# A decoder layer on one Trainium2 core: moving one operand load and fixing the order of splits in the direct parts of the last product

## Chip, core and metric

The kernel runs on one core of one Trainium2 chip. The metric is the device time of one execution in microseconds (us). A core has five engines that matter here: PE (TensorE, matrix products), DVE (VectorE), ACT (ScalarE), POOL (GpSimd) and SP (SyncE); each works through a queue of its own, and DMA transfers are issued from the SP and POOL queues.

## What is computed

One layer with three token mixers, an output projection, then a SwiGLU feed-forward network (FFN), on 512 positions of width 2048, in float32. Only the FFN matters for the change:

```python
def swiglu(h, w_in, w_out):
    gate, up = jnp.split(h @ w_in, 2, axis=-1)
    return (jax.nn.silu(gate) * up) @ w_out
...
        x = x + mix.astype(x.dtype)
        x = x + swiglu(rmsnorm(x, norm2_g[l]), w_ffn_in[l], w_ffn_out[l]).astype(x.dtype)
    return rmsnorm(x, final_g)
```

The hidden width is 44 tiles of 128 (5632). `h @ w_in` is called the first product here, the product with `w_out` the second.

## The kernel before

**Split operands.** Every float32 operand x of a product is cast to a rounded `hi` (on ACT) and a remainder `lo = x - hi` (on DVE). A product tile is then three matmuls, hi·hi, hi·lo and lo·hi (`mm3`), so no matmul of a weight tile can finish before its ACT cast and its DVE subtraction.

**First product.** Hidden tiles 0 and 1 (`Direct`) come first, then the loop over `Unit(j)`, j = 2 to 43. A unit makes seven combined products (a Strassen-like scheme), p1, p5, p6, p3, p7, p2, p4 in that order, and its last instructions are, on ACT, the copy of the p4 result (L924), and on DVE the add (L925) and the multiply (L926). The activations of tiles 0, 1, 2, 19, 20, 21 and 38 to 43 go to DRAM as `actd`; those of tiles 3 to 18 and 22 to 37 go there as combined operands `opd[0]` and `opd[1]`.

**Second product.** It runs over the hidden tiles in this order:

- `rest(R0, 0)`: the direct part of hidden tiles 0, 1, 2. For each pair n, n+1 of the 16 output tiles a weight block `rw` is loaded, split by `w_split` into `wh` and `wl`, and used in 2 x 18 matmuls of 256 columns into the PSUM tiles `rb`. For this first part the result is copied into `acc` by ACT (L1026); later parts add to `acc` on DVE (L1028).
- `load_ops(0)`: 14 pieces of the combined operands, each a DMA `so<-opd` on the POOL queue, a cast (L1000, ACT) and a subtraction (L1001, DVE) into `fop`. Then eight times `second(q, 3)`: seven combined products each.
- `rest(R1, 19)`, `load_ops(1)`, eight times `second(q, 22)`: the same for the other half; here the result of `rest` is added on DVE.
- `load_rest(R2)` and `last(n, ...)`: the direct part of hidden tiles 38 to 43, with the final norm.

`load_rest(js)` loads activations: a DMA `st<-actd` on POOL, a cast to `ra` (L990, ACT) and a subtraction (L991, DVE).

**Buffers.** The raw weights `rw` and half of the raw weights of `second` share three buffers (tag `w`); `wh` and `wl` have three each; the staging tiles of the pieces alternate between tags `raw` (three) and `s` (two); the staging tiles of `load_rest` have two (`rs`) and one (`sm`); `fop` tiles take over the space of the units' operands in the order in which the last unit frees them.

**Order of the queues.** Nothing in this part of the program writes the order out by hand. A scheduler orders each engine's queue from data dependences, buffers and a priority by program order, so an instruction whose inputs are ready can be queued ahead of earlier ones of the program. The queues are worked through in the order so found. `tc.keep_in_program_order(ins)` adds one edge: `ins` is queued behind the instruction that stands just before it in the program on the same engine. It adds no wait of its own on that one's end, other than the place in the queue.

Of the kernel before, what the change touches and what calls it, by code (L numbers as in the profile page):

```python
# [8 lines left out]
F32 = mybir.dt.float32  # L9
F32R = mybir.dt.float32r  # L10
# [6 lines left out]
P = 128  # L17
# [6 lines left out]
TH = T // 2  # L24
GP = 8
R0 = (0, 1, 2)
S0 = 3
R1 = (19, 20, 21)
# [21 lines left out]
def group_of(j):  # L50
    return 0 if S0 <= j < S0 + 2 * GP else 1 if S1 <= j < S1 + 2 * GP else None
# [40 lines left out]
def trunk_kernel(  # L92
# [22 lines left out]
    act, dve, pool = nc.scalar, nc.vector, nc.gpsimd  # L115
# [42 lines left out]
    def mm3(out, lh, ll, rh, rl, start, stop, skip=False):  # L158
        pe.matmul(out, lhsT=lh, rhs=rh, start=start, stop=False, skip_group_check=skip)
        pe.matmul(out, lhsT=lh, rhs=rl, start=False, stop=False, skip_group_check=skip)  # L160
        pe.matmul(out, lhsT=ll, rhs=rh, start=False, stop=stop, skip_group_check=skip)
# [546 lines left out]
    wq = tc.alloc_tile_pool(name="wq", bufs=1)  # L708
    x1 = keep.tile([P, KT, T], F32, tag="k", name="x1")
    x1d = [dram.tile([P, T], F32, name=f"x1d{n}") for n in range(KT)]  # L710
    actd = {j: dram.tile([P, 2, TH], F32, name=f"actd{j}") for j in range(NH) if group_of(j) is None}
# [23 lines left out]
    def op_pair(pi, b):  # L735
        t = pair_tile(nop[0], f"op{pi}")
        nop[0] += 1
        act.copy(t[:, :, 0], b)
        dve.tensor_sub(t[:, :, 1], b, t[:, :, 0].bitcast(F32))
        ops[pi] = t  # L740
# [3 lines left out]
    def rms2(th):  # L744
        hs = HALF[th]
        pb = big.tile([P, T], F32, tag="b", name=f"rms2_{th}")[:, :TH]
        pe.matmul(pb, lhsT=onesD, rhs=sqb[:, hs], start=True, stop=True)
        act.activation(rs2[:, hs], pb, AF.Sqrt, bias=eps)
        dve.reciprocal(rs2[:, hs], rs2[:, hs])
# [37 lines left out]
    sm = wq.tile([P, 3 * TH], F32, tag="sm", name="sm")  # L787
# [70 lines left out]
    class Unit(Products):  # L858
# [61 lines left out]
        def p4(self):  # L920
# [9 lines left out]
            elif self.pos:  # L930
# [4 lines left out]
                dve.tensor_sub(pr[:, 3], pr[:, 1], pr[:, 5])  # L935
                pool.dma_start(opd[g][(self.j - (S0, S1)[g]) // 2], pr[:, 0:7])

    rms2(1)
    big.release()
    pz = tc.alloc_tile_pool(name="pz", bufs=2, space=PSUM)  # L940
# [14 lines left out]
    dve.tensor_sub(b21, b21, b11)  # L955
    op_pair(4, b21)
    for j in range(2, NH):
        u = Unit(j)
        u.load1()
        u.load3()  # L960
        u.load2()
        for st in ("p1", "p5", "p6", "p3", "p7", "p2", "p4"):
            getattr(u, st)()
# [4 lines left out]
    fops = {}  # L968
    for i, pi in enumerate((1, 2, 5, 3, 6, 7, 4)):
        fops[pi] = pair_tile(i, f"fop{pi}")  # L970
    PORDER = (1, 5, 6, 3, 7, 2, 4)
    nst = [0]

    def stage():
        nst[0] += 1
        tg, bufs = ("rs", 2) if nst[0] % 3 else ("sm", 1)
        return wq.tile([P, 2, TH], F32, tag=tg, bufs=bufs, name=f"st{nst[0]}")

    acts = {}

    def load_rest(js):
        for i, j in enumerate(js):
            st = stage()
            pool.dma_start(st, actd[j])
            if len(js) == 3:
                ra = wq.tile([P, 2, 2, TH], F32R, tag="ld", bufs=3, name=f"ra{j}")
                hi, lo = ra[:, 0], ra[:, 1]
            else:
                hi, lo = (fops[PORDER[e // 8]][:, e % 8] for e in (2 * i, 2 * i + 1))
            act.copy(hi, st)  # L990
            dve.tensor_sub(lo, st, hi.bitcast(F32))  # L991
            acts[j] = (hi, lo)

    def load_ops(g):
        for pi in PORDER:
            for i, tg, bufs in ((0, "raw", 3), (4, "s", 2)):
                st = wq.tile([P, 1024], F32, tag=tg, bufs=bufs, name=f"so{g}{pi}{i}").rearrange("p (a t) -> p a t", t=TH)
                pool.dma_start(st, opd[g][i:i + 4, :, pi - 1].rearrange("a p t -> p a t"))
                hi, lo = (fops[pi][:, i:i + 4, x] for x in range(2))
                act.copy(hi, st)  # L1000
                dve.tensor_sub(lo, st, hi.bitcast(F32))  # L1001

    def w_split(w, cols, name):
        wh = wp.tile([P, 1024], F32R, tag="wh", name=f"wh_{name}")[:, :cols]
        wl = wp.tile([P, 1024], F32R, tag="wl", name=f"wl_{name}")[:, :cols]
        act.copy(wh, w)
        dve.tensor_sub(wl, w, wh.bitcast(F32))
        return wh, wl

    def rest(js, base):  # L1010
        kw = len(js)
        for n in range(0, KT, 2):
            w = wp.tile([P, 1024], F32, tag="w", name=f"rw{base}_{n}")[:, :2 * kw * P]
            nc.sync.dma_start(w.rearrange("p (n c) -> p n c", n=2),
                              wf2[n:n + 2, :, base:base + kw].rearrange("n p k c -> p n (k c)"))
            wh, wl = w_split(w, 2 * kw * P, f"r{base}_{n}")
            for i in range(2):
                tg = "bbzyxzyx"[(n + i) % 8]
                b = {"b": p2, "z": pz}.get(tg, pa).tile([P, T], F32, tag=tg, name=f"rb{base}_{n}{i}")
                for h in range(2):  # L1020
                    for kk in range(kw):
                        c = slice((i * kw + kk) * P, (i * kw + kk + 1) * P)
                        ah, al = acts[js[kk]]
                        mm3(b[:, HALF[h]], wh[:, c], wl[:, c], ah[:, h], al[:, h], kk == 0, kk == kw - 1)
                if base == 0:
                    act.copy(acc[:, n + i], b)  # L1026
                else:
                    dve.tensor_add(acc[:, n + i], acc[:, n + i], b)  # L1028

    GW = GP * P  # L1030

    def second(q, base):
# [12 lines left out]
        def prod(pi, a, out, start, dst):  # L1045
            wh, wl = w_split(a, GW, f"s{nm}_{pi}")
            o = fops[pi]
            for k in range(GP):
                c = slice(k * P, k * P + P)
                mm3(out, wh[:, c], wl[:, c], o[:, k, 0], o[:, k, 1], start and k == 0, k == GP - 1, skip=True)  # L1050
            d = acc[:, dst[0], HALF[dst[1]]]
            dve.tensor_add(d, d, out)
# [22 lines left out]
                dve.tensor_add(acc[:, n], acc[:, n], xr)  # L1075
        prod(4, a22, bx, False, (n2, 0))

    load_rest(R0)
    rest(R0, 0)
    load_ops(0)  # L1080
    for q in range(KT // 2):
        second(q, 3)
        if q == 3:
            load_rest(R1)
    rest(R1, 19)
    load_ops(1)
    for q in range(KT // 2):
        second(q, 22)
    load_rest(R2)

    sqf = wq.tile([P, 1024], F32, tag="raw", bufs=3, name="sqf")[:, :T]
# [32 lines left out]
    def last(n, th):  # L1124
# [5 lines left out]
        if th is None:  # L1130
            wh, wl = w_split(w, LW, f"f{n}")
        else:
            m = n - WIDE
            both = fops[PORDER[2 + m // 2]].rearrange("p k w t -> p (k w t)")
            wh, wl = (both[:, (2 * (m % 2) + x) * LW:(2 * (m % 2) + x + 1) * LW] for x in range(2))
            if th == 0:
                act.copy(wh, w)
                dve.tensor_sub(wl, w, wh.bitcast(F32))
# [21 lines left out]
    for th in range(2):  # L1160
        for n in range(WIDE, KT):
# [3 lines left out]
            if th == 1 and n > WIDE:  # L1165
                f = 4 * (n - WIDE - 1)
# [75 lines left out]
```

## Time and profile before

| | us |
|---|---|
| median of 3 runs | 2120.89 (2120.11 to 2120.92) |
| the profiled execution | 2120.17 |
| its span in the trace | 2118.5 |

The span is what the trace covers; 1.7 us of the execution lie around it. PE is busy in nearly every slice of the page. In the trace, a matmul's record is longer than its turn, because matmuls overlap; the distance between the starts of neighbours is what one costs. A row that names an idle time in brackets says how long the engine stood still before it and what ended that. The granted clock (PEclk) is given as a share of 2.4 GHz, so 0.5 is 1.2 GHz.

### The profile page before, as it was taken

The numbers are of one execution on the slowest core, as the hardware profiler recorded it, in microseconds if no ns is written. First come the engines' busy times: TensorE is split into PE (matmuls) and PEld (weight loads), VectorE is DVE, ScalarE is ACT, GpSimd is POOL, SyncE is SP. The second block draws the span as 40 slices with busy tenths as digits, with TensorE's granted clock in tenths as the row PEclk, the third lists the DMA queues.
The fourth block names the chain that finished last, engine by engine and source line by source line (L and its number), as shares of the span: only waits on it lengthen the run. The fifth ranks groups of instructions, "written<-read, shape, count | busy, mean of one in ns | idle before, by whom it ended". The sixth has DMA issues, their size and how long they took to land.

```text
span 2118.5 us, 32060 instructions
## 1 busy us (share of the span) xinstructions
PE 2098.1 (99%) x12770; PEld 1887.8 (89%) x12770; DVE 1604.2 (76%) x2183; ACT 1055.0 (50%) x1467; POOL 113.3 (5%) x212
## 2 busy tenths in 40 slices
PE   9999999999999999999999999999999999999997
PEld 8988899888888898888888888888888999999997
DVE  6445655566576779888988888888888788887765
ACT  6334455566655555445445444444545534533344
POOL 3000000000012210000000000000001000200000
PEclk9999999999999999999999999999999999999999
DMA  6332222222277764343344343343335645643333
GB/s 212 85 108 81 73 75 92 70 70 80 70 241 232 239 195 163 122 137 135 119 135 141 113 137 127 125 137 132 129 120 162 196 132 156 214 151 100 108 93 115
DMA packets 87670, 281.90 MB, mean 133 GB/s; under 512 B 10544, under 2 KB 25056, under 8 KB 87520
## 3 DMA queue, kind: packets, MB, share of 16 engines
q1 hardware_dynamic: 73088, 228.75, 33.5%
q0 software_dynamic: 13216, 50.34, 7.0%
q8 instruction: 100, 1.64, 0.3%
q10 hardware_dynamic: 1216, 0.76, 0.1%
q14 instruction: 50, 0.41, 0.1%
HBM read 253.60 MB, written 26.21 MB: 132 GB/s over the span
## 4 chain that ended last, share of the span: by engine, by line
PE 86%; issue 9%; DVE 1%; DMA 1%; ACT 1%; POOL 0%; DVEq 0%; POOLq 0%; ACTq 0%
PE bx L70 16%; PE sx L70 9%; PE wo L70 8%; PE bz L70 8%; PE wsd L70 6%; PE sz L70 4%; PE wsg L70 4%; PE by L70 4%; PE b L70 3%; PE c L70 3%; PE rb L70 2%; PE sy L70 2%; PE a L70 2%; PE wsr L70 2%; PE wsu L70 2%
## 5 line engine op out<-in xcount | busy, mean ns | idle before, releaser
L70 PE MATMUL bx<-op,fh 128*128 128x512 f32 x1344 | 478.0, 395 | 1.1 <-ACT fh L811 1.1
L70 PE MATMUL bx<-op,fl 128*128 128x256 f32 x1344 | 379.3, 282 | 0.9 <-DVE fl L812 0.9
L70 PEld LDWEIGHTS bx<-op,fh 128*128 128x128 f32 x1344 | 252.4, 188 | 60.1 <-ACT fh L811 1.4
L811 ACT CAST fh<-s 128x1024 fp32r<-128x1024 f32 x168 | 176.9, 1053 | 191.9 <-PE bx L70 59.1
L70 PEld LDWEIGHTS bx<-op,fl 128*128 128x128 f32 x1344 | 253.1, 188 | 1.2 <-DVE fl L812 1.2
L70 PE MATMUL bz<-op,fh 128*128 128x512 f32 x672 | 240.5, 396 | 0.0
L812 DVE TENSOR_TENSOR fl<-s,fh 128x1024 fp32r<-128x1024 f32 x168 | 204.9, 1220 | 43.3 <-ACT fh L811 43.2
L811 ACT CAST fh<-f 128x1024 fp32r<-128x1024 f32 x126 | 132.5, 1052 | 167.2 <-PE bx L70 85.4
L70 PE MATMUL bz<-op,fl 128*128 128x256 f32 x672 | 189.5, 282 | 0.2 <-DVE fl L812 0.2
L70 PE MATMUL sx<-fop,wh_s 128*128 128x256 f32 x1024 | 185.0, 282 | 0.0
L70 PE MATMUL wo<-mxs,wh_o 128*128 128x512 f32 x512 | 180.3, 394 | 1.6 <-ACT wh_o L154 1.6
L812 DVE TENSOR_TENSOR fl<-f,fh 128x1024 fp32r<-128x1024 f32 x126 | 153.8, 1220 | 15.6 <-ACT fh L811 15.2
L70 PEld LDWEIGHTS sx<-fop,wh_s 128*128 128x128 f32 x1024 | 157.8, 189 | 0.0
L70 PEld LDWEIGHTS bz<-op,fh 128*128 128x128 f32 x672 | 126.3, 188 | 30.5
L70 PE MATMUL wo<-mxs,wl_o 128*128 128x256 f32 x512 | 144.7, 283 | 0.0
L70 PE MATMUL sx<-fop,wl_s 128*128 128x256 f32 x512 | 144.3, 282 | 0.0
L70 PEld LDWEIGHTS bz<-op,fl 128*128 128x128 f32 x672 | 126.6, 188 | 0.5 <-DVE fl L812 0.5
L70 PE MATMUL wsd<-xs,wh_d 128*128 128x512 f32 x384 | 122.8, 401 | 0.0
L70 PE MATMUL by<-op,fh 128*128 128x512 f32 x336 | 119.9, 397 | 0.0
L70 PEld LDWEIGHTS wo<-mxs,wh_o 128*128 128x128 f32 x512 | 96.2, 188 | 24.0 <-ACT wh_o L154 2.0
L70 PEld LDWEIGHTS sx<-fop,wl_s 128*128 128x128 f32 x512 | 96.8, 189 | 0.0
L70 PEld LDWEIGHTS wo<-mxs,wl_o 128*128 128x128 f32 x512 | 96.3, 188 | 0.5 <-DVE wl_o L155 0.3
(406 smaller groups left out, 4720.7 us busy)
## 6 DMA issues: line engine op xcount, KB each, us to landing
f<-wf SPq DMA_DIRECT2D x168, 512.0 KB, 3.9
w_o<-wout SPq DMA_DIRECT2D x36, 512.0 KB, 4.3
sraw<-wf SPq DMA_DIRECT2D x32, 512.0 KB, 3.9
sw<-wf SPq DMA_DIRECT2D x32, 512.0 KB, 4.3
w2o<-wout SPq DMA_DIRECT2D x28, 512.0 KB, 4.7
opd<-tmp POOLq DMA_DIRECT2D x16, 896.0 KB, 4.1
so<-opd POOLq DMA_DIRECT2D x28, 512.0 KB, 5.2
w_d<-wst SPq DMA_DIRECT2D x24, 512.0 KB, 3.5
```

What stands on the lines that cost most here:

```text
L70: self.note(self.tc.nc.tensor.matmul(out, lhsT=lhsT, rhs=rhs, **k), out, rhs)
L811: act.copy(wh, a)
L812: dve.tensor_sub(wl, a, wh.bitcast(F32))
```

## The change

`load_rest` moves ahead of the units, and `load_rest(R0)` is called ahead of unit 19 (`S0 + 2 * GP`) and no longer behind the last unit. The cast and the subtraction of `load_rest`, of `load_ops` and of the `w_split` of `rest` go through `pin`, which is `keep_in_program_order`. `load_ops` becomes a generator of its 14 pieces, and `rest` takes one piece ahead of the matmuls of each of its 16 output tiles. The `w_split` calls of `second` and `last` stay as they were.

```diff
+    def load_rest(js):
+        for i, j in enumerate(js):
+            st = stage()
+            pool.dma_start(st, actd[j])
...
+            pin(act.copy(hi, st))
+            pin(dve.tensor_sub(lo, st, hi.bitcast(F32)))
+            acts[j] = (hi, lo)
+
+    pin = tc.keep_in_program_order
     rms2(1)
...
     for j in range(2, NH):
+        if j == S0 + 2 * GP:
+            load_rest(R0)
         u = Unit(j)
...
     def load_ops(g):
         for pi in PORDER:
             for i, tg, bufs in ((0, "raw", 3), (4, "s", 2)):
...
-                act.copy(hi, st)
-                dve.tensor_sub(lo, st, hi.bitcast(F32))
-
-    def w_split(w, cols, name):
+                pin(act.copy(hi, st))
+                pin(dve.tensor_sub(lo, st, hi.bitcast(F32)))
+                yield
+
+    def w_split(w, cols, name, hold=lambda ins: ins):
...
-        act.copy(wh, w)
-        dve.tensor_sub(wl, w, wh.bitcast(F32))
+        hold(act.copy(wh, w))
+        hold(dve.tensor_sub(wl, w, wh.bitcast(F32)))
         return wh, wl
 
-    def rest(js, base):
+    def rest(js, base, pieces):
...
-            wh, wl = w_split(w, 2 * kw * P, f"r{base}_{n}")
+            wh, wl = w_split(w, 2 * kw * P, f"r{base}_{n}", pin)
             for i in range(2):
+                next(pieces, None)
...
+        for _ in pieces:
+            pass
...
-    load_rest(R0)
-    rest(R0, 0)
-    load_ops(0)
+    rest(R0, 0, load_ops(0))
...
-    rest(R1, 19)
-    load_ops(1)
+    rest(R1, 19, load_ops(1))
```

## Rows read from the trace of the kernel before

**Rows 1.** The page, busy us of each engine, share of the span, instructions.
```profile
PE 2098.1 (99%) x12770; PEld 1887.8 (89%) x12770; DVE 1604.2 (76%) x2183; ACT 1055.0 (50%) x1467; POOL 113.3 (5%) x212
```
**Rows 2.** Waits of PE, whole span: us in total, times, longest.
```profile
PE wo L70 <- ACT wh_o L154: 1.6, 1, 1.6
...
PE bx L70 <- ACT fh L811: 1.1, 1, 1.1
...
PE bx L70 <- DVE fl L812: 0.9, 1, 0.9
```
**Rows 3.** Timeline of PE: first matmuls of both direct parts, and what follows them.
```profile
1644.27 0.40 PE L70 MATMUL rb<-ra,wh_r 128*128 128x256 f32 x2
...
1682.27 0.40 PE L70 MATMUL sx<-fop,wh_s 128*128 128x256 f32 x2
...
1842.48 0.40 PE L70 MATMUL rb<-ra,wh_r 128*128 128x256 f32 x2
...
1877.03 0.40 PE L70 MATMUL sx<-fop,wh_s 128*128 128x256 f32 x2
```
**Rows 4.** Timeline of PE around its wait in the first direct part.
```profile
1665.73 0.28 PE L70 MATMUL rb<-ra,wl_r 128*128 128x256 f32 x1
1666.97 0.50 PE L70 MATMUL rb<-ra,wh_r 128*128 128x256 f32 x2 [0.96 <-ACT wh_r L1006]
1667.97 0.45 PE L70 MATMUL rb<-ra,wl_r 128*128 128x256 f32 x1 [0.49 <-DVE wl_r L1007]
```
**Rows 5.** Timeline of ACT, then of DVE, at the same place.
```profile
1664.66 1.05 ACT L1000 CAST fop<-so 128x1024 fp32r<-128x1024 f32 x1 [2.94 <-DMA so<-opd]
1665.61 0.58 ACT L1026 COPY acc<-rb 128x512 f32<-128x512 f32 x1
1666.09 0.83 ACT L1006 CAST wh_r<-rw 128x768 fp32r<-128x768 f32 x1
...
1666.95 0.96 DVE L1007 TENSOR_TENSOR wl_r<-rw,wh_r 128x768 fp32r<-128x768 f32 x1
```
**Rows 6.** Windows: stretch, length, busy us (count) of PE, PEld, DVE, ACT, POOL, then PEclk, DMA share, GB/s.
```profile
590.00:595.00 5.00, 3.36 (x19) 2.85 (x19) 4.70 (x7) 1.71 (x3) 0.73 (x2) 1.00 1.00 382
...
850.00:860.00 10.00, 8.94 (x52) 7.54 (x51) 8.94 (x11) 5.83 (x8) 0.00 (x0) 1.00 0.23 88
1149.30:1168.99 19.69, 19.69 (x113) 17.19 (x113) 17.23 (x21) 9.77 (x13) 0.53 (x1) 1.00 0.43 153
...
1668.00:1670.00 2.00, 2.00 (x10) 2.00 (x11) 2.00 (x2) 2.00 (x4) 0.00 (x0) 0.54 0.63 131
```
**Rows 7.** Timelines of DVE and ACT at the load of R0, early units.
```profile
818.62 0.68 DVE L991 TENSOR_TENSOR ra<-st,ra 128x512 fp32r<-128x512 f32 x1
...
850.08 0.62 ACT L990 CAST ra<-st 128x512 fp32r<-128x512 f32 x1 [4.42 <-DMA st<-actd]
```
**Rows 8.** Timelines, hand-over from PE to DVE and steps of ACT and DVE.
```profile
2011.46 0.40 PE L70 MATMUL sy<-fop,wh_s 128*128 128x256 f32 x2
...
2011.66 0.42 DVE L1052 TENSOR_TENSOR acc<-acc,sx 128x256 f32<-128x256 f32 x1 [0.66 <-PE sx L70]
...
1871.51 1.28 DVE L1028 TENSOR_TENSOR acc<-acc,rb 128x512 f32<-128x512 f32 x2
...
1647.76 0.35 ACT L924 COPY tmp<-bx 128x256 f32<-128x256 f32 x1
```
**Rows 9.** DMA issues: size and median us to landing; then the SP queue.
```profile
so<-opd POOLq DMA_DIRECT2D x28, 512.0 KB, 5.2
...
st<-actd POOLq DMA_DIRECT2D x12, 256.0 KB, 3.0
...
1667.94 0.33 SPq L1037 DMA_DIRECT2D sw<-wf  x1
```
**Rows 10.** Timelines at the start of the last direct part: DVE's subtractions of R2, PE.
```profile
2028.13 1.29 DVE L991 TENSOR_TENSOR fop<-st,fop 128x512 fp32r<-128x512 f32 x2
...
2037.20 0.63 PE L70 MATMUL fb_None<-fop,wh_f 128*128 128x512 f32 x2
```

More of the change, by code (lines that the diff above doesn't have):

```diff
@@ L936, in p4, with stage @@
                 pool.dma_start(opd[g][(self.j - (S0, S1)[g]) // 2], pr[:, 0:7])
+    nst = [0]
+    def stage():
+        nst[0] += 1
+        tg, bufs = ("rs", 2) if nst[0] % 3 else ("sm", 1)
+        return wq.tile([P, 2, TH], F32, tag=tg, bufs=bufs, name=f"st{nst[0]}")
+    acts = {}
+    def load_rest(js):
+        for i, j in enumerate(js):
+            st = stage()
+            pool.dma_start(st, actd[j])
+            if len(js) == 3:
+                ra = wq.tile([P, 2, 2, TH], F32R, tag="ld", bufs=3, name=f"ra{j}")
+                hi, lo = ra[:, 0], ra[:, 1]
+            else:
+                hi, lo = (fops[PORDER[e // 8]][:, e % 8] for e in (2 * i, 2 * i + 1))
+            pin(act.copy(hi, st))
+            pin(dve.tensor_sub(lo, st, hi.bitcast(F32)))
+            acts[j] = (hi, lo)
+    pin = tc.keep_in_program_order
     rms2(1)
@@ L971, in trunk_kernel @@
     PORDER = (1, 5, 6, 3, 7, 2, 4)
[L972 to L989, printed above, removed]
-            act.copy(hi, st)
-            dve.tensor_sub(lo, st, hi.bitcast(F32))
-            acts[j] = (hi, lo)
     def load_ops(g):
@@ L999, in load_ops @@
                 hi, lo = (fops[pi][:, i:i + 4, x] for x in range(2))
-                act.copy(hi, st)
-                dve.tensor_sub(lo, st, hi.bitcast(F32))
-    def w_split(w, cols, name):
+                pin(act.copy(hi, st))
+                pin(dve.tensor_sub(lo, st, hi.bitcast(F32)))
+                yield
+    def w_split(w, cols, name, hold=lambda ins: ins):
         wh = wp.tile([P, 1024], F32R, tag="wh", name=f"wh_{name}")[:, :cols]
         wl = wp.tile([P, 1024], F32R, tag="wl", name=f"wl_{name}")[:, :cols]
-        act.copy(wh, w)
-        dve.tensor_sub(wl, w, wh.bitcast(F32))
+        hold(act.copy(wh, w))
+        hold(dve.tensor_sub(wl, w, wh.bitcast(F32)))
         return wh, wl
-    def rest(js, base):
+    def rest(js, base, pieces):
         kw = len(js)
```

## The prediction

> **What bounds the kernel now.** I read the page first: PE is busy for 2098.1 us of 2118.5 [rows 1], so time can only be won where PE stands still, and any new stand-still of PE costs its full length. The second view is the list of what PE waited for [rows 2] and PE's own timeline: four waits bear on this change. Two fall on the early units (bx, 1.1 and 0.9 us) [rows 2], two on the first direct part (rb, 0.96 and 0.49) [rows 4]. The third view is PE's timeline at the ends of the two direct parts [rows 3]. They hold the same 288 matmuls. The second one takes 1877.03 - 1842.48 = 34.55 us, 0.12 us a matmul, without a gap; the first takes 1682.27 - 1644.27 = 38.00. So the first loses 3.45 us, and the second nothing. The fourth view, ACT's and DVE's timelines at the wait [rows 4, 5], tells why: ACT stood 2.94 us before a piece's cast whose DMA had not landed; behind it in ACT's queue were a copy of a result and the cast of the next weights, and PE needed that cast.
>
> **What the wait of before teaches about size.** ACT runs copy of acc, cast of wh, and DVE then the subtraction of wl [rows 4, 5]. From the copy's start to the cast's is 0.48 us, from the cast's start to PE's first matmul 0.88, from the cast's start to PE's first matmul with wl 1.88. PE's last matmul ahead of it started at 1665.73 and took 0.12, so its turn ended at 1665.85; it went on with wl at 1667.97, with two matmuls (0.24) done in between: 1.88 us lost. The other 3.45 - 1.88 = 1.57 went to the clock: 0.54 granted behind this wait [rows 6], near the 1.2 GHz level. A wait of 1.6 us elsewhere was followed by no fall (1.00 granted in 590 to 595), nor were those of 0.9 and 1.1 us [rows 2, 6].
>
> **The change, part by part.**
>
> *The load of R0, moved to unit 19.* In the early units it goes from ACT and DVE. ACT's 4.42 us stand at the cast of ra [rows 7], which ended in PE's wait of 1.1, is gone: -1.06. The subtraction at 818.62 stood ahead of a weight's subtraction for which PE waited 0.9; 0.6 of it goes [rows 2, 7]: -0.58. At unit 19 three casts and three subtractions are added, 0.62 and 0.68 each [rows 7]: 3 x 0.62 = 1.9 us of ACT and 2.0 of DVE. A unit there is 19.69 us with DVE busy for 17.23 and ACT for 9.77 [rows 6], so 2.4 us of DVE are free: I put it at zero, at most 0.7 if two subtractions come just ahead of a needed one. The three DMAs stay free to be issued early, and POOL has time (5% busy) [rows 1]; the staging buffers are held until unit 19, and the loads that follow in them are needed only in the second product: zero.
>
> *The waits of the first direct part* go: in a fixed order the weights' cast no longer stands behind a piece that is late by several us. -3.45, at least -1.7 if a piece still comes late. All gains: 3.45 + 1.06 + 0.58 = 5.1 us, bounds 5.1 and 3.4.
>
> *The pinned splits of the first direct part.* Here is the price. In the program, the ACT instruction just before the cast of the weights of pair n+2 is the copy of result n+1 into acc (L1026). Pinned behind it, the cast of wh stands in ACT's queue behind a copy that waits for PE to finish tile n+1. So PE has run out of split weights at each of the seven borders between pairs, and nobody prefetches across. From the end of PE's turn: 0.20 until the consumer starts (PE goes on at 2011.46, DVE starts at 2011.66 [rows 8]), 0.48 for the copy, 1.88 from cast to PE's matmul with wl: 2.56. In it PE can run what needs wh alone: two matmuls (0.24) of this tile and two of the other tile of the pair: 0.48. A border costs 2.56 - 0.48 = 2.08. Bounds: 1.60 if the second half of both tiles gives another four matmuls, 2.32 if the other tile gives nothing. The opening is alike: the first cast is pinned behind unit 43's L924, its subtraction behind L926. 0.20 + 0.25 (the copy of 0.35 [rows 8], a tenth overlapped) + 1.88 = 2.33, less 0.48 = 1.85 (1.37 to 2.09). Could another product fill the waits? Those of second() need raw weights in the `w` buffers, which go to all eight rw first; before, the first sw left SP at 1667.94, over 23 us into that part [rows 3, 9]. In the new order, that buffer comes free with the sixth split, so a product of second() is ready for the last border only. Sum: 1.85 + 6 x 2.08 = 14.3 us, bounds 1.37 + 5 x 1.60 = 9.4 and 2.09 + 7 x 2.32 = 18.3. The pieces themselves are no longer late: five are staged ahead, more than two pairs of over 4 us each, against 5.2 to land [rows 9].
>
> *The pinned splits of the second direct part.* Results are added by DVE there, so ACT's casts run ahead, but the subtraction of wl is pinned behind the add of result n+1. 0.20 + 0.60 (an add's start to the next one's: two take 1.28, one of them the 0.68 of its full length [rows 8]) + 1.02 (DVE's start of wl to PE, 1666.95 to 1667.97 [rows 4, 5]) = 1.82, less 0.48 = 1.34 (0.86 to 1.58). The opening stands behind the shorter add of second(): 0.20 + 0.33 + 1.02 - 0.48 = 1.07 (0.59 to 1.31). Sum with six borders: 1.07 + 6 x 1.34 = 9.1 us, bounds 0.59 + 5 x 0.86 = 4.9 and 1.31 + 7 x 1.58 = 12.4. Before, this part had no wait at all [rows 3].
>
> *The loads of R1 and R2.* R1's pinned pairs stand inside second(), with time ahead: zero. R2's first subtraction is pinned behind the last add of second(7, 22), which waits for PE; before, all six were done by 2029.4, ahead of PE's start at 2037.20 [rows 10]. Now 0.20 + 0.33 + 0.73 - 0.23 (one matmul runs before it) = 1.0. Three staging buffers hold six tiles: the fourth load starts when the first subtraction is done, 3.0 to land [rows 9], then cast and subtraction, 1.3: PE reaches that tile after 2.1 us and stands, unless it runs the next output tile's first three K tiles meanwhile: 0.3 or 2.4 more. 1.3 to 3.4; nothing shows which, I take the middle, 2.3.
>
> *The clock.* Sixteen waits of 1 to 2 us, each able to cost 1.57 more [rows 3, 4, 6]. The nearest rows, 1.45 us idle with a fall and 1.6 without, stand one to one for the seven uncovered waits of the first part: 3.5 x 1.57 = 5.5. For the second part's shorter waits I take none, as behind 0.9 and 1.1. Bounds 0 and 16 x 1.57 = 25.1.
>
> The Trainium skill (TensorE: Matmul & The Clock Gate, "Why this matters for your kernels") lets the clock fall only after idle gaps longer than any of those worked out here; the fall in the 1668 to 1670 row differs from that. By it the clock term would be zero.
>
> **Sum.** 14.3 + 9.1 + 2.3 + 5.5 - 5.1 = +26.1 us on the profiled execution's 2120.17: 2146.3, rounded to 2146; that execution lies 0.7 under the median of the runs, which is within the rounding. Bounds: 9.4 + 4.9 + 1.3 - 5.1 = +10.5 (2131) and 18.3 + 12.4 + 3.4 + 25.1 - 3.4 = +55.8 (2176).
>
> **Rivals.** (1) The clock stays up at every border: 2146 - 5.5 = 2141; the rows at 1.00 speak for it, the 0.54 row against it [rows 6]. The rule of the Trainium skill named above would give this case too. (2) It falls at every border, because here the waits come every 6 us and not once: 26.1 - 5.5 + 25.1 = +45.7, 2166; no row shows a series of waits. (3) On the other side: faster. PE's queue is not pinned, and if the scheduler finds other matmuls for each wait, only the gains are left: 2120.17 - 5.1 = 2115. The place is PE's order inside `rest`; it decides from 2.3 us of foreign matmuls at each border on (one product of second() is 24 x 0.12 = 2.9 us and would do). Against it stands the order of the buffers [rows 9]. (4) The pins do not bind, because the queues would have come out so anyhow: only the move of the load acts, 2120.17 - 1.6 = 2118.5. Against it: before, pieces, copies and casts do not stand in that fixed order [rows 5], and the second part ran without a gap, which the pinned order can't give.
>
> **How the numbers follow.** Forecast 2146 (its own range 2136 to 2156): 0.45. Rival 1: 0.20. Rival 2: 0.15. Rival 3: 0.10. Rival 4: 0.07. 0.03 for more than the bounds. A measurement of this kernel tells about 0.2%, 4.2 us, from no change. Slower: 0.45 + 0.20 + 0.15 + 0.03 = 0.83; same 0.07; faster 0.10. The range reaches from just under the lower bound, 2128, to above rival 2, 2168, and leaves out rivals 3 and 4 and the rest.
>
> **What would show it.** Right: PE's timeline in both direct parts with a wait every 36 matmuls, ended in the first by ACT's cast and then DVE's subtraction, in the second by the subtraction alone; the first part over 48 us from first to last matmul, the second over 40; ACT's copy of acc directly ahead of each weight cast; no wait of PE in the early units. Wrong: weight casts ahead of the copy; rb matmuls broken up by those of sx; a direct part of 35 us. The clock term shows as granted clock under 1.00 in these stretches alone.

## The result and the profile after

The changed kernel takes 2152.64 us (median of 4 runs, 2150.82 to 2154.11), 1.0149 times the time of before, interval [1.0136, 1.0162]: 32 us slower. Its profiled execution took 2150.82 us with a span of 2149.1, against a span of 2118.5 before, so the two traces are 30.6 us apart.

The page first, the row that answers to [rows 1]:

```profile
PE 2107.4 (98%) x12770; PEld 1890.9 (88%) x12770; DVE 1607.9 (75%) x2183; ACT 1055.0 (49%) x1467; POOL 110.8 (5%) x212
```

PE runs the same 12770 instructions. Its busy time grows by 9.3 us of the 30.6; the rest is standing still. (A matmul's record of 0.28 is longer than its turn of 0.12 and counts in full ahead of a stop, and at the lower clock a record is 0.41; so busy time grows a little with stops.) The list of what PE waited for, whole span, in us in total, times and longest, shows where:

```profile
PE rb L70 <- ACT wh_r L1010: 16.0, 13, 1.6
PE rb L70 <- DVE wl_r L1011: 4.6, 10, 1.6
...
PE fb_None L70 <- ACT fop L956: 1.5, 2, 1.1
PE fb_None L70 <- DVE fop L957: 0.9, 2, 0.6
```

Of [rows 2], the wait of `bx` for ACT is gone, and in the same list the one for DVE is 0.5 in place of 0.9. The matmuls of the direct parts (`rb`) wait 23 times, 20.6 us together, where they waited twice before, 1.45 us [rows 4]. New are four waits of the last direct part (`fb`), 2.4 us, and two of products of `second` that PE began inside the direct parts, 1.0 us.

**The first direct part**, PE's timeline (start, duration of the record; in brackets the idle time before it and what ended it). It answers to [rows 3, 4]:

```profile
1642.49 0.28 PE L70 MATMUL bx<-op,fl 128*128 128x256 f32 x1
1643.96 0.74 PE L70 MATMUL rb<-ra,wh_r 128*128 128x256 f32 x4 [1.19 <-ACT wh_r L1010]
1645.02 0.39 PE L70 MATMUL rb<-ra,wl_r 128*128 128x256 f32 x1 [0.32 <-DVE wl_r L1011]
...
1648.83 0.28 PE L70 MATMUL rb<-ra,wl_r 128*128 128x256 f32 x1
1650.52 0.74 PE L70 MATMUL rb<-ra,wh_r 128*128 128x256 f32 x4 [1.41 <-ACT wh_r L1010]
...
1658.50 0.74 PE L70 MATMUL rb<-ra,wh_r 128*128 128x256 f32 x4 [1.41 <-ACT wh_r L1010]
1659.49 0.38 PE L70 MATMUL rb<-ra,wl_r 128*128 128x256 f32 x1 [0.25 <-DVE wl_r L1011]
1659.71 0.40 PE L70 MATMUL rb<-ra,wh_r 128*128 128x256 f32 x2
...
1664.99 0.74 PE L70 MATMUL rb<-ra,wh_r 128*128 128x256 f32 x4 [1.41 <-ACT wh_r L1010]
...
1693.04 0.74 PE L70 MATMUL rb<-ra,wh_r 128*128 128x256 f32 x4 [1.41 <-ACT wh_r L1010]
1693.99 0.50 PE L70 MATMUL sx<-fop,wh_s 128*128 128x256 f32 x2 [0.21 <-ACT wh_s L1010]
1694.73 0.39 PE L70 MATMUL rb<-ra,wl_r 128*128 128x256 f32 x1 [0.24 <-DVE wl_r L1011]
...
1698.67 0.28 PE L70 MATMUL sx<-fop,wl_s 128*128 128x256 f32 x1
```

PE reaches this part at 1642.49 + 0.12 = 1642.61, 1.66 us earlier than before, and leaves it at 1698.67: 56.06 us, where the 288 matmuls at 0.12 need 34.56. At every border between two pairs PE stands 1.41 us for the cast and runs the four matmuls that need `wh` alone (x4). At the first five it then stands another 0.25 or 0.26 for the subtraction and goes on; the last two are told below. The borders at 1658.50 and 1664.99 are 6.49 apart, where 36 matmuls need 4.32: 2.17 us are lost at one, more than the two idle times, mostly because these begin only where the longer records end. ACT's and DVE's timelines at the first border (compare [rows 5]) show what the cast stood behind:

```profile
1649.15 0.58 ACT L1031 COPY acc<-rb 128x512 f32<-128x512 f32 x1 [0.34 <-PE rb L70]
1649.63 0.83 ACT L1010 CAST wh_r<-rw 128x768 fp32r<-128x768 f32 x1
...
1650.49 0.96 DVE L1011 TENSOR_TENSOR wl_r<-rw,wh_r 128x768 fp32r<-128x768 f32 x1 [0.43 <-ACT wh_r L1010]
```

ACT's queue was free 0.34 us before the copy and waited for PE's last matmul of the pair. The cast of the next weights needs nothing of that pair, but its place is behind the copy.

**The second direct part**, PE's timeline, then DVE's at its first border:

```profile
1858.60 1.71 PE L70 MATMUL rb<-ra,wh_r 128*128 128x256 f32 x12
1860.14 0.39 PE L70 MATMUL rb<-ra,wl_r 128*128 128x256 f32 x1
...
1865.89 0.39 PE L70 MATMUL rb<-ra,wl_r 128*128 128x256 f32 x1 [1.65 <-DVE wl_r L1011]
...
1871.58 0.74 PE L70 MATMUL rb<-ra,wh_r 128*128 128x256 f32 x4 [1.59 <-ACT wh_r L1010]
...
1904.72 0.28 PE L70 MATMUL sx<-fop,wl_s 128*128 128x256 f32 x1
```

```profile
1864.28 0.69 DVE L1033 TENSOR_TENSOR acc<-acc,rb 128x512 f32<-128x512 f32 x1
1864.89 0.95 DVE L1011 TENSOR_TENSOR wl_r<-rw,wh_r 128x768 fp32r<-128x768 f32 x1
```

1904.72 - 1858.60 = 46.12 us for 34.56 of `rb` and 0.48 of four matmuls of `second` that fill a gap: 11.1 lost, where before nothing was. Here the subtraction stands behind the add that waits for PE.

**The last direct part**, timelines of PE, of DVE and of POOL (compare [rows 10]):

```profile
2064.41 0.63 PE L70 MATMUL fb_None<-fop,wh_f 128*128 128x512 f32 x2
2065.69 0.50 PE L70 MATMUL fb_None<-fop,wh_f 128*128 128x512 f32 x1 [0.65 <-DVE fop L957]
...
2069.85 0.50 PE L70 MATMUL fb_None<-fop,wh_f 128*128 128x512 f32 x1 [0.46 <-ACT fop L956]
...
2073.31 0.49 PE L70 MATMUL fb_None<-fop,wh_f 128*128 128x512 f32 x1 [1.08 <-ACT fop L956]
```

```profile
2064.61 0.42 DVE L1059 TENSOR_TENSOR acc<-acc,sx 128x256 f32<-128x256 f32 x1 [1.15 <-PE sx L70]
2064.95 1.89 DVE L957 TENSOR_TENSOR fop<-st,fop 128x512 fp32r<-128x512 f32 x3
...
2066.20 1.14 POOL L950 DMA_DIRECT2D st<-actd  x2 [27.36 <-DVE fop L957]
```

The subtractions of R2 begin behind the last add of `second`, at 2064.95. Before, they were done some 8 us ahead of PE [rows 10]. Only then do the staging buffers come free for the other three loads.

**Where the 30.6 us are.** Early units -1.66; first direct part 56.06 - 34.56 - 0.24 (two matmuls of `second` in it) = 21.26 lost against 3.45 before: +17.8; second direct part +11.1; last direct part, up to the end of its last `fb_None` record, 2109.01 - 2064.41 = 44.60 against 41.02: +3.6; the rest -0.2.

### The profile page after: what moved, and what is told of

Same layout as the page of the kernel before. It is cut to its first block, busy times and chain, and to the rows that moved or that the text cites. A ratio compares the mean times of both kernels' runs of the same rounds, so it can differ in the third digit from the quotient of the medians.

```text
span 2149.1 us, 32074 instructions
## 1 busy us (share of the span) xinstructions
PE 2107.4 (98%) x12770; PEld 1890.9 (88%) x12770; DVE 1607.9 (75%) x2183; ACT 1055.0 (49%) x1467; POOL 110.8 (5%) x212
## 3 DMA queue, kind: packets, MB, share of 16 engines
q8 instruction: 100, 1.64, 0.3%
## 4 chain that ended last, share of the span: by engine, by line
PE 95%; DVE 2%; issue 2%; ACT 1%; DMA 0%; POOL 0%; DVEq 0%; POOLq 0%; ACTq 0%
PE bx L70 22%; PE bz L70 11%; PE wo L70 8%; PE sx L70 8%; PE wsd L70 6%; PE by L70 5%; PE sz L70 4%; PE wsg L70 4%; PE b L70 3%; PE c L70 3%; PE sy L70 2%; PE rb L70 2%; PE a L70 2%; PE wsr L70 2%; PE wsu L70 2%; PE fb_None L70 2%
## 5 line engine op out<-in xcount | busy, mean ns | idle before, releaser
L811 ACT CAST fh<-s 128x1024 fp32r<-128x1024 f32 x168 | 176.9, 1053 | 194.7 <-PE by L70 58.5
```

What stands on the lines that cost most here:

```text
L811: act.copy(wh, a)
```

## The experiments

The theory: an instruction pinned behind one that empties a PSUM tile waits for PE, and what PE needs next stands behind it. Rivals: the pieces' loads are what is late; R2's stall is due to something else; the clock carries much of it. Unless said otherwise each edit is made to the changed kernel.

**The move alone.** All pins are off but those of the R0 load at unit 19, and no pieces stand between the tiles.

```diff
+        hold = pin if js is R0 else lambda ins: ins
...
-            pin(act.copy(hi, st))
-            pin(dve.tensor_sub(lo, st, hi.bitcast(F32)))
+            hold(act.copy(hi, st))
+            hold(dve.tensor_sub(lo, st, hi.bitcast(F32)))
...
-                pin(act.copy(hi, st))
-                pin(dve.tensor_sub(lo, st, hi.bitcast(F32)))
+                act.copy(hi, st)
+                dve.tensor_sub(lo, st, hi.bitcast(F32))
...
-            wh, wl = w_split(w, 2 * kw * P, f"r{base}_{n}", pin)
+            wh, wl = w_split(w, 2 * kw * P, f"r{base}_{n}")
             for i in range(2):
-                next(pieces, None)
```

> Of the change only the move of the load of R0 to unit 19 is kept, pinned there; splits, pieces and the other loads stand as before. Border theory (the fixed order of splits is the whole price, the move a small gain): the 1.66 us by which the first direct part began earlier (1642.61 against 1644.27), so 2120.5 - 1.7 = 2118.8, both direct parts as before (38.0 and 34.55 us from first matmul to the next stage), no wait at the last one. Rival (part of the price comes from the load in unit 19, through DVE or the staging buffers): 2120 or more, with a PE wait near 1150.

2117.79 us, 0.9987 of before [0.9976, 0.9997]. In PE's waits between 1640 and 1700 two are left:

```profile
PE rb L70 <- ACT wh_r L1011: 0.7, 1, 0.7
PE rb L70 <- DVE wl_r L1012: 0.5, 1, 0.5
```

The first part takes 36.31 us (from 1642.86), the second 35.06. So the whole loss comes with the pins and the new place of the pieces, and the move is worth 2.5 us by the medians: PE enters the first part 1.4 us earlier and spends 1.7 less in it, the second takes 0.5 more. Most of the 1.7 is the clock: here the wait of 0.7 and 0.5 was followed by a granted clock of 1.00 (1665 to 1670), where the wait of before was followed by 0.54 [rows 6]. Nothing shows that the move caused this.

**R2 free.** The pins of the last load off.

```diff
+        hold = pin if js is not R2 else lambda ins: ins
...
-            pin(act.copy(hi, st))
-            pin(dve.tensor_sub(lo, st, hi.bitcast(F32)))
+            hold(act.copy(hi, st))
+            hold(dve.tensor_sub(lo, st, hi.bitcast(F32)))
```

> The change, but the load of R2 is not pinned. My account of the last direct part (the subtractions stand behind the last add of second(), and three staging buffers hold six tiles): its 3.6 us go, 2152.6 - 3.6 = 2149.0, and PE enters the last part without a wait. Rival (the wait there comes from buffers or DMA that are late by the delays before it, not from the pin): 2152, waits on fop unchanged.

2149.20 us, 1.0137 [1.0123, 1.0151]; PE waits for nothing in the last direct part. The median is 3.4 us under that of the changed kernel, near the 3.6 of its trace. (The two profiled executions differ by 0.1 only: in this one the first direct part took 58.5 us, with three falls of the clock.)

**The splits of the direct parts free**, everything else pinned.

```diff
-            wh, wl = w_split(w, 2 * kw * P, f"r{base}_{n}", pin)
+            wh, wl = w_split(w, 2 * kw * P, f"r{base}_{n}")
```

> The change, but the weight splits of both direct parts are not pinned; pieces and loads stay pinned and alternate. Border theory: weights are split ahead again and both direct parts lose their waits: the first 36 to 40 us and not 56, the second 35 to 38 and not 46, so 2152.6 - 16 to 20 - 8 to 11 = 2121.6 to 2128.6. Rival (late pieces: the buffers of the pieces come free behind the adds, and the weight casts wait behind late pieces on ACT): the second part stays at 42 to 46 us with ACT waiting for so, 2131 to 2136.

2128.48 us, 1.0040 [1.0026, 1.0054]. The first part takes 34.54 us, which is no loss at all, and the second 36.8, with one wait behind a late piece (0.8 and 0.5 us) like the one of before: without the pins of the splits the waits at the borders are gone. But the time is at the upper edge of what was expected. PE's waits between 1640 and 2060 show one more cost:

```profile
PE sx L70 <- DVE acc L1059: 3.7, 3, 1.9
```

These waits lie in `second`, and with them two more, for an add of the direct part (1.6) and for a subtraction of weights (0.9). Its two loops become 2.5 and 4.7 us longer. With -1.8 (early units), -3.45, +2.2 (second part), +2.5, +4.7 and R2's +3.6, the sum is +7.8; the profiled execution was +7.86.

**The pieces free**, the splits still pinned.

```diff
-                pin(act.copy(hi, st))
-                pin(dve.tensor_sub(lo, st, hi.bitcast(F32)))
+                act.copy(hi, st)
+                dve.tensor_sub(lo, st, hi.bitcast(F32))
                 yield
```

> The change, but the casts and subtractions of the pieces are not pinned; splits and loads stay pinned. Border theory: nothing changes in the first direct part (56 us, 2.2 us lost at a border), and in the second the late pieces go and only the subtraction behind the add is left, 7 x 1.3 = 9 us: 2152.6 - 2 = 2150.6. Rival (late pieces are the price of the second part): it falls to 35 to 38 us, 2152.6 - 8 to 11 = 2142 to 2145. If the alternation itself were what costs, the first part would fall too, under 2140.

2166.93 us, 1.0222 [1.0208, 1.0236]: 14 us slower than the changed kernel, and none of the expectations held. ACT's timeline at the entry of the first direct part:

```profile
1646.54 1.04 ACT L1003 CAST fop<-so 128x1024 fp32r<-128x1024 f32 x1 [1.14 <-DMA so<-opd]
...
1648.02 0.35 ACT L924 COPY tmp<-bx 128x256 f32<-128x256 f32 x1
1648.28 0.83 ACT L1010 CAST wh_r<-rw 128x768 fp32r<-128x768 f32 x1
```

Free pieces float ahead of unit 43's copy (L924), each waits for its DMA, and the first weight cast is pinned behind that copy: PE stands 6.26 us at the entry. The first part takes 63.8 us and the second 57.4. So the pins of the pieces, given pinned splits, are worth some 14 us. At the entry the rows show why: pinned pieces can't come ahead of the first split. In the second part the cause is only seen in part: PE's longest wait there, 3.96 us, ended with a cast for which ACT had waited 3.14 us for the weights' own DMA, and at a granted clock of 0.91 over 57.1 us about 5 of the 11 us more are clock, by an estimate from these two numbers.

**One pair ahead.** The split of pair n+2 is written ahead of the matmuls of pair n; all pins stay.

```diff
-        for n in range(0, KT, 2):
+        def split(n):
             w = wp.tile([P, 1024], F32, tag="w", name=f"rw{base}_{n}")[:, :2 * kw * P]
...
-            wh, wl = w_split(w, 2 * kw * P, f"r{base}_{n}", pin)
+            return w_split(w, 2 * kw * P, f"r{base}_{n}", pin)
+
+        coming = split(0)
+        for n in range(0, KT, 2):
+            wh, wl = coming
+            if n + 2 < KT:
+                coming = split(n + 2)
```

> The change with all its pins, but the weights of the next pair are split ahead of the matmuls of the present pair, so that the cast is pinned one pair earlier than the copy it stood behind. Border theory: the order is as fixed as before, yet the borders close: the first direct part 36 to 38 us (only the opening is left), the second 35 to 38, the last part still 3.6 too long: 2152.6 - 18 to 20 - 8 to 11 = 2122 to 2127. Rival (a fixed order of splits and pieces costs as such, since pieces are late and weights stand behind them): the second part stays over 42 us, 2129 or more.

2125.50 us, 1.0016 [1.0007, 1.0025], as expected. PE's waits between 1630 and 2060:

```profile
PE sx L70 <- DVE wl_s L1011: 3.0, 2, 1.5
...
PE rb L70 <- ACT wh_r L1010: 1.2, 1, 1.2
```

Of all waits of `rb` the one at the opening is left; the two parts take 36.4 and 34.8 us. What is pinned is the same; only the neighbour it is pinned to has changed, from the copy of result n+1 to that of result n-1, which is done long before. That is the border theory in one edit. Left are the opening, R2 (+3.6) and 2.2 and 3.2 us in the two loops of `second`.

**One pair ahead, opening and R2 free.** The same, with the first split of each part and R2's load not pinned.

```diff
+        hold = pin if js is not R2 else lambda ins: ins
...
-            return w_split(w, 2 * kw * P, f"r{base}_{n}", pin)
+            return w_split(w, 2 * kw * P, f"r{base}_{n}", pin if n else lambda ins: ins)
```

> As the kernel with the splits one pair ahead, and the first split of each direct part and the load of R2 are not pinned. Border theory: no wait is left in either direct part nor at the last one: 34.6 and 35 to 37 us, so 2120.5 - 1.7 - 3.4 + 0 to 3 = 2115.4 to 2118.5, a little faster than the kernel before. Rival (the pieces that now come later hold up the products behind the direct part, as they did with free splits, by 2.5 and 4.7 us): 2118 to 2123, no gain.

2123.55 us, 1.0011 [1.0001, 1.0020]. The gain that the border theory promised (2115.4 to 2118.5) did not come; the time is just above the rival's 2118 to 2123. ACT's timeline:

```profile
1642.74 0.35 ACT L924 COPY tmp<-bx 128x256 f32<-128x256 f32 x1
1650.68 0.59 ACT L1038 COPY acc<-rb 128x512 f32<-128x512 f32 x1 [7.58 <-DMA so<-opd]
```

Behind L924 ACT stands 7.58 us for a piece whose load is late, with the copy of the first result behind it. The first part takes 38.6 us, and the loop of `second` that follows it 166.0 in place of 160.2.

**One pair ahead, R2 free, first split pinned.** The splits are written one pair ahead as above and all pinned; the load of R2 is not.

```diff
+        hold = pin if js is not R2 else lambda ins: ins
...
-            pin(act.copy(hi, st))
-            pin(dve.tensor_sub(lo, st, hi.bitcast(F32)))
+            hold(act.copy(hi, st))
+            hold(dve.tensor_sub(lo, st, hi.bitcast(F32)))
...
+            return w_split(w, 2 * kw * P, f"r{base}_{n}", pin)
```

> As the kernel with the splits one pair ahead and the load of R2 free, but with the first split of each direct part pinned again; beside that kernel it tells what the pin of the first split is worth. Theory (without it the first direct part starts at once but a piece stands in ACT's queue ahead of a copy and a weight cast before its DMA has landed, 7.6 us there): the first direct part is 36.4 us again, with its opening wait and no other, and the last part has none: 2125.5 - 3.5 = 2122. Rival (the opening pin only costs; the late piece has another reason): the first part stays at 38 us or more, plus the opening: 2125 or more.

2122.28 us, 1.0008 [0.9998, 1.0017]: the time of before, and what was expected. The first part takes 36.25 us. The pinned first split costs its opening wait and in return keeps the late piece behind it. By the medians of this run and the last the two can't be told apart; it is the first part, 36.25 against 38.6, that shows it.

**The copy on DVE.** In the first direct part the result goes to `acc` on DVE and no longer on ACT; all pins stay.

```diff
-                    act.copy(acc[:, n + i], b)
+                    dve.tensor_copy(acc[:, n + i], b)
```

> The change with all its pins, but the result of the first direct part is copied by DVE and not by ACT. Border theory: the cast of the next weights no longer stands behind the copy, only the subtraction does, as in the second part: a border costs 1.3 to 1.6 and not 2.2, the first direct part 44 to 47 us and not 56, 2152.6 - 9 to 12 = 2141 to 2144. Rival (the waits of the first part come from ACT's load of pieces and casts, not from the place behind the copy): 53 to 56 us, 2149 to 2153.

2141.00 us, 1.0089 [1.0073, 1.0106]. PE's waits between 1640 and 1691:

```profile
PE rb L70 <- ACT wh_r L1010: 5.5, 6, 1.6
PE rb L70 <- DVE wl_r L1011: 2.1, 5, 0.7
```

The first part takes 47.0 us, nearly the 46.1 of the changed kernel's second part (45.7 in this run), whose result always went through DVE. With the copy off ACT, the cast is no longer behind it, and the subtraction behind DVE's copy sets the price. (Why most waits still end with ACT's cast is told under the next run.) So the two parts differ by the engine that empties the tile, as the prediction had it.

**No pieces in the second direct part.** They come behind it.

```diff
-                next(pieces, None)
+                if base == 0:
+                    next(pieces, None)
```

> The change with all its pins, but the second half's pieces come behind its direct part and not in alternation with it. Asked is the second direct part alone (the products behind it will wait for the pieces, so that the time in all is over 2155). Late-piece account: ACT no longer waits for pieces ahead of a weight cast, waits ended by ACT's cast are gone and each border costs what the subtraction behind the add costs, 1.3 to 1.4 us: 34.55 + 9 to 10 = 43.6 to 44.5 and not 46.1. Pin-only account (the pieces had no part in it): 46 us and the same mix of waits.

2181.06 us, 1.0278 [1.0259, 1.0298]. The 28 us more than the changed kernel's lie behind the part, where `second` waits 22.6 us in one piece, since the pieces now start so late. The part itself is what was asked for, and it takes 46.0 us, as with the pieces. ACT's timeline in it, then PE's:

```profile
1864.04 0.83 ACT L1010 CAST wh_r<-rw 128x768 fp32r<-128x768 f32 x1 [4.66 <-PE rb L70]
```

```profile
1864.92 0.74 PE L70 MATMUL rb<-ra,wh_r 128*128 128x256 f32 x4 [0.81 <-ACT wh_r L1010]
...
1865.77 0.39 PE L70 MATMUL rb<-ra,wl_r 128*128 128x256 f32 x1
1865.99 0.41 PE L70 MATMUL rb<-ra,wh_r 128*128 128x256 f32 x2
...
1870.67 0.74 PE L70 MATMUL rb<-ra,wh_r 128*128 128x256 f32 x4 [0.81 <-ACT wh_r L1010]
```

The borders are 1870.67 - 1864.92 = 5.75 apart, 1.43 over the 4.32 of 36 matmuls, without a single piece in the way. In the changed kernel ACT also stood 9.29 us for a late piece in this part, which looks like a cause of it all. It is one of 0.9 us: the first two borders cost 1.92 and 1.86 there and 1.43 each here. Three later borders cost 1.1 us more here, where the weights of one pair landed late and PE had fewer matmuls at hand for the gap, so that in all 0.1 us comes back. The rows show too why PE's waits here are put down to ACT: PE's order puts the four `wh` matmuls of a later pair into the gap, and their cast needs one of the three `wh` buffers, which PE frees only at the border.

**The move with free splits one pair ahead.** Pinned is the R0 load alone.

```diff
+        hold = pin if js is R0 else lambda ins: ins
...
-                pin(act.copy(hi, st))
-                pin(dve.tensor_sub(lo, st, hi.bitcast(F32)))
+                act.copy(hi, st)
+                dve.tensor_sub(lo, st, hi.bitcast(F32))
...
-            wh, wl = w_split(w, 2 * kw * P, f"r{base}_{n}", pin)
+            return w_split(w, 2 * kw * P, f"r{base}_{n}", lambda ins: ins)
+
+        coming = split(0)
+        for n in range(0, KT, 2):
+            wh, wl = coming
+            if n + 2 < KT:
+                coming = split(n + 2)
             for i in range(2):
-                next(pieces, None)
```

> Only the load of R0 at unit 19 is pinned; splits and pieces are free, as before the change, but the weights of the next pair stand ahead of the present pair's matmuls in the program, and so have priority over pieces. Theory (what is left of the first direct part's loss, 36.3 against 34.55 us, is a weight cast behind a late piece): 2117.8 - 1.7 = 2116.1, no wait in either direct part. Rival (program order one pair earlier does not change which piece stands ahead): 2117.8, the same wait of about 0.7 and 0.5 us.

2117.51 us, 0.9982 [0.9973, 0.9991], the lowest median of all. Of PE's waits for `rb` one of 0.5 us is left between 1640 and 2090, in the second part. The first part takes 35.1 us in place of 36.3, the second 35.3 in place of 35.1. The 2116.1 of the theory is not reached: against the move alone (2117.79) the times show no difference, and the intervals overlap for the most part.

## Why the prediction was right, and where it was off

**The mechanism holds.** The prediction said that splits pinned behind result copies stop PE at every border, and that this outweighs the gains by far. Three runs bear it out from different sides: splits free, no border waits; splits pinned to a neighbour that is done early, no border waits; the copy moved to the other engine, the border cost of the second part in place of that of the first. The time is 6.6 us above the forecast, inside its range; that it comes so near is in part luck, since errors of opposite sign stand in the sum, as told below. Rival 3, that PE fills the waits, fell: at six borders of the first part PE found nothing but the four `wh` matmuls, at the seventh two more. Rival 4, that the pins do not bind, fell with the move alone, 35 us below the changed kernel.

**The move of the load**: -1.64 forecast, -1.66 measured. That the two agree to 0.02 is luck: the wait of 0.9 fell by 0.44 and not by 0.58, and with the same move PE reached the first part between 1642.44 and 1643.83 in the other runs. Zero cost at unit 19 holds in the windows view (stretch, length, then busy us and count of PE, PEld, DVE, ACT and POOL, PEclk, DMA share, GB/s), where the unit of [rows 6] is again without a gap, with DVE busy for 18.30 us:

```profile
1149.60:1169.30 19.70, 19.70 (x115) 17.20 (x114) 18.30 (x25) 10.75 (x15) 1.62 (x3) 1.00 0.52 181
```

**The border of the first part**: 2.08 forecast, 2.17 measured. The chain came out step by step: PE's turn ends at 1648.95, the copy starts 0.20 later, the cast 0.48 after it, PE's matmul with `wl` 1.88 after that, 2.56 in all, less 0.48 for four matmuls. What it lacked is 0.1 at the restart: the first matmul with `wl` has a turn of 0.22 us (1659.49 to 1659.71), not 0.12. The opening: 1.85 forecast; 1645.02 - 1642.61 - 0.48 = 1.93 measured, and 2.03 with the same 0.1 of the restart.

**The number of borders is the step that failed.** I counted six in each part, because a product of `second` should cover the last. It is seven in both. At the first part's last border PE found two matmuls of `second` (0.24 us), not a product; in the second part four (0.48). That a product's weights are loaded does not make it ready: they pass the same ACT and DVE queues. DVE's timeline at the first part's last border:

```profile
1692.58 1.23 DVE L1049 TENSOR_TENSOR s2s<-s1s,sw 128x1024 f32<-128x1024 f32 x1
1693.72 0.95 DVE L1011 TENSOR_TENSOR wl_r<-rw,wh_r 128x768 fp32r<-128x768 f32 x1
```

The combination s2s, weights for a product of `second`, stood ahead of the subtraction of `wl`, and the border cost 0.46 more than the others. The border before cost 0.61 more in the same way, behind s1s (1.23 us from 1685.39). In the sum of the first part the prediction had none of these: 2.2 for the seventh border, 1.1 for the two delays and 0.7 for the restarts.

**The second part's border**: 1.34 forecast, 1.43 measured, again the 0.1 of the restart; seven of them are 10.0. The first two, at 1865.89 and 1871.58, cost 0.5 and 0.4 more, because the next cast of `wh` stood behind the late piece: at the first PE had no `wh` matmuls for the gap, at the second they came late. So "no longer late" was wrong for that one piece. The opening cost only 0.2 instead of 1.07, because three pairs had been cast ahead and PE ran twelve `wh` matmuls in it. "Ended by the subtraction alone" was wrong in its label: most of these waits end with ACT's cast, because PE's order puts `wh` matmuls of a later pair into the gap. The price is the same.

**R2**: 2.3 forecast, 3.6 measured, just above my upper bound of 3.4. The wait for the first subtraction came out (1.0 forecast, 0.9 measured with its restart). PE did take the next output tile's first K tiles meanwhile, as in the cheaper case. But I counted one late load, the fourth, at the median of 3.0 [rows 9], and the sixth tile's load, the last, took 5.09 in the chain of waits:

```profile
2067.53 5.09 DMA st<-actd
```

So PE stood twice for loads, not once: 0.46 at 2069.85 for the fourth tile, and 1.08 and another 0.23 for the sixth, behind the 0.65 for the first subtractions and each with its restart. Why the last load took 2 us longer was not followed up.

**The clock**: 5.5 forecast (3.5 falls of 1.57), 3.0 measured. Two of the borders of the first part are followed by a lower granted clock, the others by 1.00:

```profile
1650.50:1658.50 8.00, 6.32 (x37) 5.91 (x37) 3.42 (x4) 3.82 (x6) 1.77 (x3) 0.79 0.58 183
1658.50:1665.00 6.50, 4.84 (x37) 4.43 (x37) 3.40 (x4) 3.80 (x6) 1.30 (x3) 1.00 0.72 222
...
1678.00:1686.00 8.00, 6.34 (x37) 5.93 (x37) 3.95 (x4) 3.82 (x6) 0.62 (x1) 0.79 0.57 201
```

Those two periods are 7.98 and not 6.49 us long: 1.49 each, against the 1.57 worked out from before, which holds the 0.1 of a restart too. Half of seven waits was the wrong count by one and a half; the price of one was right. The count is no fixed property of this order: with the same pins in the first part the run with R2 free had three falls, behind the opening and the fourth and sixth border, and the run without pieces in the second part one, behind the sixth. The second part had none (1.00 throughout), as I took it. Rival 1 (no fall) and rival 2 (at every border) are both out. (Of the waits of before that were followed by no fall, the one of 0.9 us has no window in [rows 6]; its trace has 1.00 there too, from 815 to 825.) The Trainium skill (TensorE: Matmul & The Clock Gate, "Why this matters for your kernels") names only longer idle gaps as what brings the clock down. Five of the seven borders agree with that and two do not; there the measurement decides.

**The sum again**: early units -1.6 forecast and -1.66 measured; first part 14.3 + 5.5 - 3.45 = +16.4 and +17.8; second +9.1 and +11.1; R2 +2.3 and +3.6; rest 0 and -0.2. Three terms are too low, by counts or prices of steps that were in the sum, apart from DVE's two delays and the restarts, which were not in it. The first part comes as near as 1.4 us only because the clock term was 2.5 too high where the waits were 4.0 too low.

What stays open: why `second` waits for DVE's adds and subtractions when the splits run ahead and the pieces keep their pins (1.4 to 5.8 us in each loop in those runs). The move alone and the last run, with free splits and free pieces, do not show it. One trace hints at the pinned pieces: with the splits free, DVE stood 1.46 us at 1677.54 for the cast of a piece whose DMA was late (ACT had waited 2.12 us for it), and behind that piece the work for the products of `second`, the adds of their results among it, followed without a pause on DVE until 1686. No run tested this.

## What to carry to other kernels

An instruction held behind its program neighbour inherits that neighbour's wait. Before pinning preparation work for the next tile, look at what stands just ahead of it on its engine: if it empties the accumulator of the current tile, the preparation starts only when PE has run dry. Written one pair earlier, the same pin cost nothing at the borders. And compare with the free order, not only with a partly pinned one: given pinned splits, pinning the pieces too was worth 14 us, yet both pinned together were 35 us slower than neither (the move alone).

## What the runs showed of the hardware

After a stop, PE lost another 0.1 us: the first matmul had a turn of 0.22 us in place of 0.12 (1659.49, and 1865.77 in the run without pieces), at a granted clock of 1.00. And the same idle time (1.41 and 0.25 us in a period of 36 matmuls) was followed by a granted clock of 0.79 over 8 us in two stretches and of 1.00 in others. The rows of PE ahead of the two kinds look alike, and with the same order in two other runs the falls stood at other borders.
